# Low parts of the weights kept in DRAM from the first pass for the third

## The chip, the cores and the metric

The kernel runs on one core of a Trainium2 chip. The metric is the device time of one execution in microseconds. A core has five engines with queues of their own, each in order: TensorE (PE; its weight loads are shown as PEld), VectorE (DVE), ScalarE (ACT), GpSimd (POOL) and SyncE (SP). SyncE issues the ordinary transfers, GpSimd the indexed ones (gathers); the engines wait for each other and for transfers on semaphores.

## The reference

One decoder layer on `x` of 1024 tokens by 1024 columns, all in float32:

```
h = x + mixer(rms_norm(x))          # proj = xn @ w_in (3592 columns); gated conv, gated delta rule; @ w_out
h = h + cross(rms_norm(h), mem)     # q = xn @ w_xq, 4 heads over 256 memory tokens, @ w_xo
h = h + peer(rms_norm(h))           # q = xn @ w_pq; per token 8 heads x 16 of 16384 experts:
                                    #   sum_e gate_e * gelu(x . u_e) * v_e
out = rms_norm(h)
```

The delta rule is a recurrence over tokens, in blocks of 128. `expert_u` and `expert_v` have 16384 rows of 1024 numbers.

## The kernel before

**Products in two parts.** A float32 product is made of three matmuls in fp32r: with each operand split into a high part (its value rounded to fp32r) and a low part (the rest), `mm3` (L246) adds high x high (L248), and two products of a high with a low part (L249, L250). `load_w` (L237) brings one weight piece of 128 x 1024 numbers, 512 KB: SyncE loads it to `wraw` (L240), ScalarE copies it to `whi` (L242), VectorE subtracts, `wlo = wraw - whi` (L244). There are three `wraw` buffers, two `whi` and two `wlo`. A `whi` or `wlo` buffer comes free when the matmuls that read it are done; a `wraw` buffer when the copy and the subtraction are.

**Tokens in three passes.** `Chunk` ca is tokens 0 to 255 (two blocks), cb 256 to 767 (four), cc 768 to 1023 (two). Each pass reads the same weights: `inproj` 28 pieces of `w_in`, by `proj_ct` (L302); `outproj` 8 pieces of `w_out` and the end of `cross` 8 of `w_xo`, both by `split_proj` (L331) and `proj_tok` (L314); `cross` 8 pieces of `w_xq`; `queries` 8 of `w_pq`. That is 60 pieces in each pass. Between `inproj` and `outproj` lies the recurrence (`invert`, `recur`). The keys and values of the memory, `kmd` and `vmd`, are made once, during the first pass, and loaded again by `cross`.

**Experts in two ways.** For tokens 256 to 767 the layer is computed densely: `densify` (L1025) makes a table of gates for all experts from one-hot rows (VectorE L1050, L1051, L1053; TensorE L1059; ScalarE L1063; stored to `gd` by SyncE, L1066), and `dense` (L1068) runs over all 16384 experts, loading pieces of `u_t` and `expert_v` through `load_w`. For the other four blocks the chosen rows are gathered: 128 gathers of 128 rows of `expert_u` a block (L918, `gathered`), each reduced by VectorE (L935), then as many of `expert_v`, added by VectorE (L1020), or for block 0 by TensorE (L964, L971). They land in six `g` buffers.

**Order.** The program is written as generators that `merge` interleaves in given proportions: ca alone with the memory; cb with gathers; then `queries(cb)` with the start of cc; then the rest of cc with the tables of `densify`; at last `dense` with the gathers that are left. Buffers are handed out in that order. A planner then puts each engine's instructions into a fixed order, by a priority from the program's order (shifted by the offsets `PG1`, `PG2` and so on) and by simulated times; semaphores follow from the data. On the chip each queue keeps that order, SyncE's transfers included.

Of the kernel before, what the change touches and what calls it, by code (L numbers as in the profile page):

```python
# [9 lines left out]
F32 = mybir.dt.float32  # L10
# [10 lines left out]
P = 128  # L21
SEQ = 1024
D = 1024
KD = D // P
T = 512
# [17 lines left out]
G1, G2, G3, G4, G5 = 98, 90, 107, 17, 60  # L43
A5 = -1
C4, T5 = 61, 92
NSHORT, NRAW, NHI, NLO, NG, LU, LV, VD = 6, 3, 2, 2, 6, 1, 1, 194
PG1, PG2, PG3, PT, PR, PD = 100, -25, 0, 0, 0, 0


# [63 lines left out]
def _body(ctx, tc, I, out, dbg, front_only):  # L113
    nc = tc.nc
# [12 lines left out]
    dr = ctx.enter_context(tc.tile_pool(name="dr", bufs=1, space=bass.MemoryType.DRAM))  # L127
# [9 lines left out]
    def short():  # L137
        return dp.tile([P, T + 4], F32, name="d_s")
# [6 lines left out]
    def psum():  # L145
        banks["n"] += 1
        return pp.tile([P, T], F32, name="ps" if banks["n"] % 2 or not banks["both"] else "po")
# [14 lines left out]
    cs = constants()  # L162
# [55 lines left out]
    xnd = dr.tile([SEQ, D], F32, name="xnd")  # L218
    yd = dr.tile([SEQ, D], F32, name="yd")
    gd = dr.tile([T // 32, P, P, 32], F32, name="gd")  # L220


    def rsqrt(dst, ss, scale, eps, tag=""):
# [10 lines left out]
            tt(t, t, x, op=OP.mult)  # L234
            stt(dst if it == 2 else y, t, 1.5, y, op0=OP.add, op1=OP.mult)

    def load_w(src):  # L237

        raw = wp.tile([P, D], F32, name="wraw", bufs=NRAW)
        nc.sync.dma_start(raw if len(src.shape) == 2 else raw.rearrange("p (a c) -> p a c", a=2), src)  # L240
        hi = wp.tile([P, D], F32R, name="whi", bufs=NHI)
        act(hi, raw, AF.Copy)  # L242
        lo = wp.tile([P, D], F32R, name="wlo", bufs=NLO)
        tt(lo, raw, hi.bitcast(F32), op=OP.subtract)  # L244
        return hi, lo

    def mm3(ps, lh, ll, rh, rl, first, last, open_=False):
# [19 lines left out]
    class Parts:  # L267


        def __init__(self, units, per):  # L270
            self.units, self.per = units, per
# [27 lines left out]
                stt(xlo[:, k, :nt], ps[:, :nt], gain[:, k:k + 1], xhi[:, k, :nt].bitcast(F32),  # L299
                    op0=OP.mult, op1=OP.subtract)  # L300

    def proj_ct(src, x, nt):  # L302

        xhi, xlo = x
        ps = psum()
        hi, lo = load_w(src)
        for k in range(KD):
            js = slice(k * P, (k + 1) * P)
            mm3(ps[:, :nt], hi[:, js], lo[:, js], xhi[:, k, :nt], xlo[:, k, :nt], k == 0, k == KD - 1)
            if k % 4 == 3:  # L310
                yield
        return ps[:, :nt]

    def proj_tok(wsrc, lhs, nblk, consume):  # L314

        for half in range(2):
            pss = [psum() for b in range(nblk)]
            for k in range(KD):
                cs = slice(half * 512, (half + 1) * 512)
                if k % 2 == 0:  # L320
                    hi, lo = load_w(wsrc[k * P:(k + 2) * P, cs].rearrange("(a p) c -> p a c", a=2))
                ks = slice((k % 2) * 512, (k % 2 + 1) * 512)
                xh, xl = lhs(k)
                for b in range(nblk):
                    bs = slice(b * P, (b + 1) * P)
                    mm3(pss[b], xh[:, bs], xl[:, bs], hi[:, ks], lo[:, ks], k == 0, k == KD - 1)
                yield
            for b in range(nblk):
                consume(b, half, pss[b])

    def split_proj(wsrc, units, hv):  # L331

        nt = len(hv) * P
        xhi, xlo = split_parts(nt)
        for k in range(KD):
            src = units[k // 4][:, k % 4]
            act(xhi[:, k], src, AF.Copy)
            tt(xlo[:, k], src, xhi[:, k].bitcast(F32), op=OP.subtract)
        yield

        def put(b, half, ps):
            dst = hv[b][:, half * 512:(half + 1) * 512]
            tt(dst, ps, dst, op=OP.add)

        yield from proj_tok(wsrc, lambda k: (xhi[:, k], xlo[:, k]), len(hv), put)


    def memory():
# [23 lines left out]


    class Chunk:
        def __init__(self, b0, nb):
            self.b0, self.nb, self.t0, self.T = b0, nb, b0 * P, nb * P

        def half(self):
# [20 lines left out]
    def inproj(c):  # L399

        t0, NB, T = c.t0, c.nb, c.T
# [7 lines left out]
        x = split_parts(T)  # L409
        xhi, xlo = x  # L410
# [36 lines left out]
        for i in (1, 0, 2):  # L447
            dst_u = c.half()
            qkv.append(dst_u)
            for h in range(NH):  # L450
                j = 4 * i + h
                ps = yield from proj_ct(I["w_in"][12 + j], x, T)
                raw = short()[:, :T + 3]
                nc.vector.tensor_copy(raw[:, 0:3], halo_q[:, j])
                act(raw[:, 3:T + 3], ps, AF.Copy)
                nc.vector.tensor_copy(halo_q[:, j], raw[:, T:T + 3])
                a = dst_u[:, h]
                act(a, raw[:, 0:T], AF.Copy, scale=dw[:, j, 0:1])
                for k in range(1, 4):
                    stt(a, raw[:, k:T + k], dw[:, j, k:k + 1], a, op0=OP.mult, op1=OP.add)  # L460
                th = raw[:, 0:T]
                act(th, a, AF.Tanh, scale=0.5)
                stt(a, th, 1.0, a, op0=OP.add, op1=OP.mult)
                yield
# [33 lines left out]
        cb = c.small("cb")  # L498
# [13 lines left out]

        yc = c.half()
        for j in range(4):
            pc = yield from proj_ct(I["w_in"][4 + j], x, T)
            csb = short()[:, :T]
            act(csb, pc, AF.Copy)
            ph = yield from proj_ct(I["w_in"][8 + j], x, T)
            ch = short()[:, :T + 2]
            nc.vector.tensor_copy(ch[:, 0:2], halo_c[:, j])  # L520
            tt(ch[:, 2:T + 2], csb, ph, op=OP.mult)
            nc.vector.tensor_copy(halo_c[:, j], ch[:, T:T + 2])
            yield
            a = yc[:, j]
            act(a, ch[:, 0:T], AF.Copy, scale=cw[:, j, 0:1])
            stt(a, ch[:, 1:T + 1], cw[:, j, 1:2], a, op0=OP.mult, op1=OP.add)
            stt(a, ch[:, 2:T + 2], cw[:, j, 2:3], a, op0=OP.mult, op1=OP.add)
            pb = yield from proj_ct(I["w_in"][j], x, T)
            tt(yc[:, j], a, pb, op=OP.mult)
            yield  # L530

        zT = c.half()
        for h in range(NH):
            ps = yield from proj_ct(I["w_in"][24 + h], x, T)
            th = short()[:, :T]
            act(th, ps, AF.Tanh, scale=0.5)
            stt(zT[:, h], th, 1.0, ps, op0=OP.add, op1=OP.mult)
            yield
# [147 lines left out]
    def outproj(c):  # L686
        t0, NB, T = c.t0, c.nb, c.T
        for b in range(4):
            dbgout("yT", c.yc[:, b], (b, slice(None), slice(t0, t0 + T)))
            dbgout("yT", c.yd[:, b], (4 + b, slice(None), slice(t0, t0 + T)))  # L690
        c.h = rows(NB)
        for b in range(NB):
            nc.sync.dma_start(c.h[b], I["x"][t0 + b * P:t0 + (b + 1) * P])
        yield from split_proj(I["w_out"], [c.yc, c.yd], c.h)
        for b in range(NB):
            dbgout("h1", c.h[b], slice(t0 + b * P, t0 + (b + 1) * P))


    def cross(c):
        NB, T = c.nb, c.T  # L700
        hv = c.h
# [4 lines left out]
        x = split_parts(T)  # L706
        to_channels(x[0], x[1], xs, g_x)
        yield
        qx, ox = [], []
        pend = []  # L710

        def query(i):
            if i % 4 == 0:
                qx.append(c.half())
            ps = yield from proj_ct(I["w_xq"][i], x, T)
            act(qx[i // 4][:, i % 4], ps, AF.Copy)

        def scores(h):
# [45 lines left out]
        for h in range(4):  # L764
# [4 lines left out]
                yield from query(2 * h + 3)  # L769
            values(h, pr)  # L770
            yield
        yield from split_proj(I["w_xo"], ox, hv)
        for b in range(NB):
            dbgout("h2", hv[b], slice(c.t0 + b * P, c.t0 + (b + 1) * P))

# [1 line left out]
    def queries(c):  # L777

        t0, NB, T = c.t0, c.nb, c.T
        hv = c.h  # L780
        rstd = normalise(hv)
        gffn = unit().rearrange("p a t -> p (a t)")[:, :D]
        nc.sync.dma_start(gffn, I["g_ffn_row"].partition_broadcast(P))
        xs = rows(NB)
        for b in range(NB):
            tb = slice(t0 + b * P, t0 + (b + 1) * P)
            nc.sync.dma_start(hd2[tb], hv[b])
            stt(xs[b], hv[b], rstd[:, b:b + 1], gffn, op0=OP.mult, op1=OP.mult)
            nc.sync.dma_start(xnd[tb], xs[b])
            dbgout("xn", xs[b], tb)  # L790
        x = split_parts(T)
        to_channels(x[0], x[1], xs, None)
        yield
        for b in range(NB):
            routes[c.b0 + b] = Route(c.b0 + b)
        for hh in range(4):
            pair = []
            keys = sp.tile([P, 2, P], F32, name="keys")
            nc.sync.dma_start(keys, I["keysT"][:, 2 * hh:2 * hh + 2])
            for i in (2 * hh, 2 * hh + 1):  # L800
                ps = yield from proj_ct(I["w_pq"][i], x, T)
                pair.append(short()[:, :T])
                act(pair[-1], ps, AF.Copy)
                yield
            for b in range(0, NB, 2):
                yield from best_keys(c.b0 + b, hh, pair, keys, b * P)
# [349 lines left out]
            yield  # L1156


    ca, cb, cc = Chunk(0, 2), Chunk(2, 4), Chunk(6, 2)

    def recurrence(c):
        for b in range(0, c.nb, 2):
# [16 lines left out]


    run(inproj(ca))
    mem = memory()
    next(mem)
# [71 lines left out]

# [10 lines left out]
```

## Time and profile before

Three runs: 3332.52, 3342.78 and 3343.30 us, median 3342.78.

| of the profiled execution | |
|---|---|
| its own time | 3335.89 us |
| span, first to last instruction | 3334.1 us |
| mean granted TensorE clock | 0.908 |
| busy: PE / DVE / ACT / POOL | 84% / 81% / 40% / 40% |
| read from and written to HBM | 838.77 MB, 48.76 MB |
| L244, all low parts | 452, 552.4 us of VectorE |
| L242, all high parts | 452, 479.9 us of ScalarE |

The page gives each engine's busy time over the whole span. As the program has stages with different limits, the rows below cut the span into stretches (times from the span's start). A row of such a view has the stretch, its length, the busy time and the number of instructions of PE, PEld, DVE, ACT and POOL, the granted clock, the mean busy share of the 16 DMA engines, and GB/s. A row of waits reads: engine, output and line that waited, what it waited for, the sum in us, how often, the longest. SPq is SyncE's queue of transfers.

### The profile page before, as it was taken

The page shows a single profiled execution, that of the slowest core. Times are in us where ns is not written, and L with a number is a line of the kernel's source. Part 1 is how long each engine was busy: PE and PEld are TensorE (multiplying, and loading weights), DVE is VectorE, ACT ScalarE, POOL GpSimd, SP SyncE. Part 2 cuts the span into 40 slices and gives each one's busy share as a digit, 9 for nine tenths or more (in the row PEclk, how much of TensorE's full clock was granted, in tenths as well). Part 3 has the DMA queues.
Part 4 walks back from the last instruction along what each step waited for, and adds up shares of the span by engine and source line. Part 5 has one row for each costly group of instructions (what it writes and reads, how often), then busy time and mean ns, then how long its engine had stood idle before and what let it go on. Part 6 is the DMA issues. An engine that isn't in the chain of part 4 may idle for free.

```text
span 3334.1 us, 42650 instructions
## 1 busy us (share of the span) xinstructions
PE 2784.7 (84%) x14826; PEld 2307.0 (69%) x14826; DVE 2693.7 (81%) x5527; ACT 1339.8 (40%) x2367; POOL 1324.6 (40%) x1028
## 2 busy tenths in 40 slices
PE   7898588877888877466777999999999999999950
PEld 7887466666555656465656888888888888888840
DVE  6654899978655788997668999888888888887888
ACT  5444333322232323334443554444444444444430
POOL 0000046746545441000000456556655555665665
PEclk9999788989998888788788999999999999999975
DMA  4344368959988884113455889999999999999998
GB/s 166 113 147 140 120 233 302 354 184 324 328 309 306 308 291 155 64 77 143 154 190 188 297 307 363 347 344 346 345 336 342 348 348 349 343 339 339 348 329 315
DMA packets 325495, 890.34 MB, mean 267 GB/s; under 512 B 27424, under 2 KB 96672, under 8 KB 321184
## 3 DMA queue, kind: packets, MB, share of 16 engines
q0 software_dynamic: 147456, 536.94, 44.3%
q1 hardware_dynamic: 177824, 350.69, 30.0%
q8 instruction: 116, 1.90, 0.2%
q14 instruction: 99, 0.81, 0.1%
HBM read 838.77 MB, written 48.76 MB: 266 GB/s over the span
## 4 chain that ended last, share of the span: by engine, by line
PE 43%; DVE 3%; issue 2%; DMA 1%; ACT 1%; POOL 1%; SPq 0%; POOLq 0%; DVEq 0%; ACTq 0%
PE ps L248 7%; PE ps L249 7%; PE ps L250 7%; PE po L248 7%; PE po L250 7%; PE po L249 7%; DMA g<-expert_v,g_ii 1%; POOL g L918 1%; DVE unit L1053 0%; DMA d_s<-kmd 0%; PE ps L1059 0%; DVE g_y L1020 0%; DVE wlo L244 0%; ACT whi L242 0%; DVE unit L1050 0%
## 5 line engine op out<-in xcount | busy, mean ns | idle before, releaser
L918 POOL DMA_INDIRECT g<-expert_u,g_ii x512 | 666.4, 1302 | 898.9 <-DVE t_s L820 434.4
L918 POOL DMA_INDIRECT g<-expert_v,g_ii x384 | 518.5, 1350 | 930.8 <-ACT g L1001 536.0
L242 ACT ACTIVATE whi<-wraw 128x1024 fp32r<-128x1024 f32 x452 | 479.9, 1062 | 836.0 <-PE ps L249 413.5
L244 DVE TENSOR_TENSOR wlo<-wraw,whi 128x1024 fp32r<-128x1024 f32 x452 | 552.4, 1222 | 321.7 <-ACT whi L242 319.4
L935 DVE SCALAR_TENSOR_TENSOR g<-g,xn 128x1024 f32<-128x1024 f32 x512 | 617.4, 1219 | 121.0 <-DMA g<-expert_u,g_ii 111.7
L250 PE MATMUL ps<-unit,wlo 128*128 128x512 f32 (+1 forms) x1784 | 653.3, 367 | 39.4 <-DVE wlo L244 39.3
L248 PE MATMUL ps<-unit,whi 128*128 128x512 f32 (+1 forms) x1784 | 659.1, 370 | 13.7 <-ACT whi L242 5.5
L249 PE MATMUL ps<-unit,whi 128*128 128x512 f32 (+1 forms) x1784 | 651.6, 365 | 0.0
L1020 DVE SCALAR_TENSOR_TENSOR g_y<-g,g_a,g_y 128x1024 f32<-128x1024 f32 x381 | 488.1, 1281 | 20.1 <-DMA g<-expert_v,g_ii 12.7
L249 PE MATMUL po<-wlo,unit 128*128 128x512 f32 x1136 | 444.0, 391 | 0.0
L250 PE MATMUL po<-whi,unit 128*128 128x512 f32 x1136 | 443.9, 391 | 0.0
L250 PEld LDWEIGHTS ps<-unit,wlo 128*128 128x128 f32 x1784 | 350.3, 197 | 98.6 <-DVE wlo L244 45.0
L248 PEld LDWEIGHTS ps<-unit,whi 128*128 128x128 f32 x1784 | 351.6, 197 | 76.7 <-ACT whi L242 11.0
L249 PEld LDWEIGHTS ps<-unit,whi 128*128 128x128 f32 x1784 | 351.5, 197 | 50.0 <-issue 0.8
L248 PE MATMUL po<-whi,unit 128*128 128x512 f32 x1136 | 383.1, 391 | 0.0
L249 PEld LDWEIGHTS po<-wlo,unit 128*128 128x128 f32 x1136 | 214.1, 188 | 48.3 <-issue 2.7
L250 PEld LDWEIGHTS po<-whi,unit 128*128 128x128 f32 x1136 | 214.0, 188 | 46.8 <-issue 2.5
L248 PEld LDWEIGHTS po<-whi,unit 128*128 128x128 f32 x1136 | 214.0, 188 | 45.8 <-issue 1.1
L1113 ACT ACTIVATE unit<-po 128x512 f32<-128x512 f32 x256 | 152.6, 597 | 150.1 <-PE po L250 144.8
L964 POOL DMA_INDIRECT g<-expert_v,g_y x128 | 139.4, 1089 | 161.3 <-DVE g L935 57.5
L1100 ACT ACTIVATE po<-unit 128x512 f32<-128x512 f32 x248 | 144.5, 605 | 0.0
L1059 PE MATMUL ps<-unit 128*128 128x128 f16 x1024 | 86.8, 239 | 52.3 <-DVE unit L1053 38.7
(391 smaller groups left out, 4053.1 us busy)
## 6 DMA issues: line engine op xcount, KB each, us to landing
wraw<-u_t SPq DMA_DIRECT2D x128, 512.0 KB, 7.1
wraw<-expert_v SPq DMA_DIRECT2D x128, 512.0 KB, 7.0
wraw<-w_in SPq DMA_DIRECT2D x84, 512.0 KB, 4.6
gd<-unit SPq DMA_DIRECT2D x32, 1024.0 KB, 5.9
unit<-gd SPq DMA_DIRECT2D x32, 1024.0 KB, 15.1
wraw<-w_out SPq DMA_DIRECT2D x24, 512.0 KB, 4.2
wraw<-w_xq SPq DMA_DIRECT2D x24, 512.0 KB, 4.4
wraw<-w_xo SPq DMA_DIRECT2D x24, 512.0 KB, 4.9
```

Of the source, the lines that this page charges most:

```text
L242: act(hi, raw, AF.Copy)
L244: tt(lo, raw, hi.bitcast(F32), op=OP.subtract)
L248: nc.tensor.matmul(ps, lh, rh, start=first, stop=False, skip_group_check=open_)
L249: nc.tensor.matmul(ps, lh, rl, start=False, stop=False, skip_group_check=open_)
L250: nc.tensor.matmul(ps, ll, rh, start=False, stop=last, skip_group_check=open_)
L918: nc.gpsimd.indirect_dma_start(out=g, out_offset=None, in_=I[table], in_offset=bass.IndirectOffsetOnAxis(ap=ii[:, k:k + 1], axis=0))
L935: stt(g, g, 1.0, xn, op0=OP.mult, op1=OP.mult, accum_out=r.a[:, k:k + 1])
L964: nc.gpsimd.indirect_dma_start(out=g, out_offset=None, in_=I["expert_v"], in_offset=bass.IndirectOffsetOnAxis(ap=iT[:, t:t + 1], axis=0))
L1020: stt(y, g, a[:, k:k + 1], y, op0=OP.mult, op1=OP.add)
L1059: nc.tensor.matmul(ps[:, u * P:(u + 1) * P], part[i][:, g, :, t], oj[:, g, :, t], start=i == 0, stop=i == 1)
L1100: act(pss[b], y[b][:, half * 512:(half + 1) * 512], AF.Copy)
L1113: act(y[b][:, half * 512:(half + 1) * 512], pss[b], AF.Copy)
```

## The change

`load_w` gets a key: a pass and the name of the piece. In the first pass ("save") the low part is stored, after the subtraction, into a DRAM tile `lod` of 60 slots, by SyncE. In the third pass ("use") there is no subtraction; the low part is loaded from its slot into `wlo` by SyncE. The second pass, the memory's weights and the dense stage have no key and do as before. There are four `wraw` and four `wlo` buffers instead of three and two; `whi` keeps two. For the 12 KB a partition that they take, the area of the on-chip memory that the program sets aside for its dynamic DMAs (the gathers) is given as 4096 bytes a partition.

```diff
-NSHORT, NRAW, NHI, NLO, NG, LU, LV, VD = 6, 3, 2, 2, 6, 1, 1, 194
+NSHORT, NRAW, NHI, NLO, NG, LU, LV, VD = 6, 4, 2, 4, 6, 1, 1, 194
...
+    lod = dr.tile([60, P, D], F32, name="lod")
...
-    def load_w(src):
+    parts_of = {}
+
+    def load_w(src, key=None):
...
         lo = wp.tile([P, D], F32R, name="wlo", bufs=NLO)
+        keep, *piece = key or (None,)
+        if keep == "use":
+            nc.sync.dma_start(lo.bitcast(F32), lod[parts_of[tuple(piece)]])
+            return hi, lo
         tt(lo, raw, hi.bitcast(F32), op=OP.subtract)
+        if keep == "save":
+            n = parts_of.setdefault(tuple(piece), len(parts_of))
+            nc.sync.dma_start(lod[n], lo.bitcast(F32))
         return hi, lo
...
-    def proj_ct(src, x, nt):
+    def proj_ct(src, x, nt, key=None):
...
-    def proj_tok(wsrc, lhs, nblk, consume):
+    def proj_tok(wsrc, lhs, nblk, consume, key=None):
...
-                    hi, lo = load_w(wsrc[k * P:(k + 2) * P, cs].rearrange("(a p) c -> p a c", a=2))
+                    hi, lo = load_w(wsrc[k * P:(k + 2) * P, cs].rearrange("(a p) c -> p a c", a=2),
+                                    key and (*key, half, k))
...
-                ps = yield from proj_ct(I["w_in"][12 + j], x, T)
+                ps = yield from proj_ct(I["w_in"][12 + j], x, T, (c.keep, "w_in", 12 + j))
...
-    ca, cb, cc = Chunk(0, 2), Chunk(2, 4), Chunk(6, 2)
+    ca, cb, cc = Chunk(0, 2, "save"), Chunk(2, 4), Chunk(6, 2, "use")
...
-    nc = bacc.Bacc("TRN2", target_bir_lowering=False, num_devices=1)
+    nc = bacc.Bacc("TRN2", target_bir_lowering=False, num_devices=1, dynamic_dma_scratch_size=4096)
```

## Rows read from the trace of the kernel before

**Rows 1.** Busy time of every engine by stretch (PE, PEld, DVE, ACT, POOL).
```profile
0.00:430.00 430.00, 347.90 (x2382) 325.08 (x2382) 286.35 (x869) 189.11 (x371) 0.20 (x4) 0.90 0.39 133
...
1050.00:1350.00 300.00, 233.24 (x1375) 183.00 (x1373) 241.79 (x918) 95.42 (x159) 105.66 (x95) 0.84 0.71 256
1350.00:1540.00 190.00, 105.80 (x846) 95.70 (x847) 177.91 (x519) 69.74 (x194) 0.00 (x0) 0.74 0.17 67
1540.00:1780.00 240.00, 176.34 (x1314) 146.96 (x1313) 166.21 (x338) 108.48 (x281) 0.00 (x0) 0.85 0.51 188
...
1850.00:3200.00 1350.00, 1350.00 (x5956) 1117.57 (x5955) 1142.39 (x1395) 655.83 (x948) 769.62 (x558) 1.00 0.95 341
3200.00:3334.00 134.00, 10.66 (x47) 8.46 (x46) 115.05 (x151) 10.97 (x19) 85.70 (x72) 0.55 0.86 310
```

**Rows 2.** Waits in 1050 to 1350 us.
```profile
DVE g L935 <- DMA g<-expert_u,g_ii: 35.1, 20, 4.3
...
PE ps L250 <- DVE wlo L244: 24.6, 7, 11.7
...
PE ps L971 <- DMA g<-expert_v,g_y: 22.4, 7, 6.3
...
DVE wlo L244 <- ACT whi L242: 15.5, 10, 4.4
```

**Rows 3.** Waits in 1540 to 1780 us, and a group of TensorE there with idle time.
```profile
DVE wlo L244 <- ACT whi L242: 44.4, 15, 6.7
...
ACT whi L242 <- PE ps L250: 33.0, 13, 5.9
...
PE ps L1059 <- DVE unit L1053: 16.3, 10, 5.9
...
PE ps L729 <- DMA d_s<-kmd: 9.4, 2, 4.8
...
L249 PE MATMUL ps<-wlo,unit 128*128 128x512 f32 x59 | 24.6, 417 | 4.0 <-DVE wlo L244 4.0
```

**Rows 4.** The subtraction L244 by stretch: VectorE busy (count), clock, DMA share, GB/s.
```profile
0.00:430.00 430.00, 95.44 (x78) 0.90 0.39 133
...
1050.00:1350.00 300.00, 47.30 (x39) 0.84 0.71 256
...
1540.00:1780.00 240.00, 34.22 (x28) 0.85 0.51 188
```

**Rows 5.** Tile wlo in a stretch of 50 us: PE, PEld, DVE, clock, DMA, GB/s.
```profile
1050.00:1100.00 50.00, 12.97 (x33) 6.00 (x32) 4.89 (x4) 0.83 0.97 375
```

**Rows 6.** Transfers by SyncE: count, KB each, median us from issue to landing.
```profile
wraw<-w_in SPq DMA_DIRECT2D x84, 512.0 KB, 4.6
...
xnd<-unit SPq DMA_DIRECT2D x8, 512.0 KB, 6.2
```

**Rows 7.** One issue in SyncE's queue: start, duration us, line.
```profile
1555.77 0.33 SPq L240 DMA_DIRECT2D wraw<-w_xq  x1
```

**Rows 8.** Waits of SyncE's queue: 0 to 430 us, then 1540 to 1780 us.
```profile
SPq L240 <- DVE wlo L244: 123.4, 47, 14.1
...
SPq L240 <- DVE wlo L244: 147.1, 20, 28.8
SPq L1066 <- ACT unit L1063: 40.4, 13, 10.9
```

**Rows 9.** Waits in the dense stage, 1900 to 3200 us.
```profile
ACT whi L242 <- PE ps L249: 227.5, 88, 3.9
...
DVE wlo L244 <- ACT whi L242: 175.1, 153, 3.3
...
ACT whi L242 <- DMA wraw<-expert_v: 18.7, 9, 5.8
```

**Rows 10.** Line L1020 by stretch, the last one: VectorE busy (count).
```profile
3200.00:3334.00 134.00, 97.37 (x76) 0.55 0.86 310
```

**Rows 11.** The longest wait in 1780 to 1850 us.
```profile
POOL g L918 <- ACT g L1001: 535.0, 1, 535.0
```

More of the change, by code (lines that the diff above doesn't have):

```diff
@@ L300, in to_channels @@
                     op0=OP.mult, op1=OP.subtract)
-    def proj_ct(src, x, nt):
+    def proj_ct(src, x, nt, key=None):
         xhi, xlo = x
         ps = psum()
-        hi, lo = load_w(src)
+        hi, lo = load_w(src, key)
         for k in range(KD):
@@ L329, in proj_tok, with split_proj @@
                 consume(b, half, pss[b])
-    def split_proj(wsrc, units, hv):
+    def split_proj(name, units, hv, keep):
         nt = len(hv) * P
@@ L343, in put @@
             tt(dst, ps, dst, op=OP.add)
-        yield from proj_tok(wsrc, lambda k: (xhi[:, k], xlo[:, k]), len(hv), put)
+        yield from proj_tok(I[name], lambda k: (xhi[:, k], xlo[:, k]), len(hv), put, (keep, name))
     def memory():
@@ L374, in _body, with __init__ @@
     class Chunk:
-        def __init__(self, b0, nb):
+        def __init__(self, b0, nb, keep=None):
+            self.keep = keep
             self.b0, self.nb, self.t0, self.T = b0, nb, b0 * P, nb * P
@@ L514, in inproj @@
         for j in range(4):
-            pc = yield from proj_ct(I["w_in"][4 + j], x, T)
+            pc = yield from proj_ct(I["w_in"][4 + j], x, T, (c.keep, "w_in", 4 + j))
             csb = short()[:, :T]
             act(csb, pc, AF.Copy)
-            ph = yield from proj_ct(I["w_in"][8 + j], x, T)
+            ph = yield from proj_ct(I["w_in"][8 + j], x, T, (c.keep, "w_in", 8 + j))
             ch = short()[:, :T + 2]
@@ L527, in inproj @@
             stt(a, ch[:, 2:T + 2], cw[:, j, 2:3], a, op0=OP.mult, op1=OP.add)
-            pb = yield from proj_ct(I["w_in"][j], x, T)
+            pb = yield from proj_ct(I["w_in"][j], x, T, (c.keep, "w_in", j))
             tt(yc[:, j], a, pb, op=OP.mult)
@@ L533, in inproj @@
         for h in range(NH):
-            ps = yield from proj_ct(I["w_in"][24 + h], x, T)
+            ps = yield from proj_ct(I["w_in"][24 + h], x, T, (c.keep, "w_in", 24 + h))
             th = short()[:, :T]
@@ L693, in outproj @@
             nc.sync.dma_start(c.h[b], I["x"][t0 + b * P:t0 + (b + 1) * P])
-        yield from split_proj(I["w_out"], [c.yc, c.yd], c.h)
+        yield from split_proj("w_out", [c.yc, c.yd], c.h, c.keep)
         for b in range(NB):
@@ L714, in query @@
                 qx.append(c.half())
-            ps = yield from proj_ct(I["w_xq"][i], x, T)
+            ps = yield from proj_ct(I["w_xq"][i], x, T, (c.keep, "w_xq", i))
             act(qx[i // 4][:, i % 4], ps, AF.Copy)
@@ L771, in cross @@
             yield
-        yield from split_proj(I["w_xo"], ox, hv)
+        yield from split_proj("w_xo", ox, hv, c.keep)
         for b in range(NB):
@@ L800, in queries @@
             for i in (2 * hh, 2 * hh + 1):
-                ps = yield from proj_ct(I["w_pq"][i], x, T)
+                ps = yield from proj_ct(I["w_pq"][i], x, T, (c.keep, "w_pq", i))
                 pair.append(short()[:, :T])
```

## The prediction

> **What bounds the kernel now.** I read the stages first, then who waits in two of them, then SyncE's queue and the transfers. [rows 1] cut the span at the places where the work changes. From 0 to 430 us the first pass runs nearly alone: TensorE 348 of 430 us busy, VectorE 286, DMA 0.39. From 430 to 1050 the second pass shares the core with the expert gathers. The third pass, 60 weight pieces, lies between 1050 and 1780 in three parts: 1050 to 1350 (stretch A: its input projection, the second pass's queries, gathers), 1350 to 1540 (recurrence, routing and `densify`; VectorE 178 of 190 us) and 1540 to 1780 (stretch B: output projection, cross attention, queries, and the rest of `densify`). From 1850 to 3200 the dense stage has TensorE at 1350 of 1350 us at full clock with DMA at 0.95. After it VectorE still has 76 gathered rows to add, 97.4 of the last 134 us. The reader is to see that no engine is full in A (TensorE 233 of 300, VectorE 242) nor in B (176 of 240, VectorE 166), so what the third pass is worth is read from the waits there.
>
> In A TensorE stands 24.6 us waiting for the low part of a weight; VectorE stands 15.5 us for the high part before it can subtract, 35.1 us for gathers, and TensorE 22.4 us for gathers [rows 2]. In B the same subtraction holds VectorE 44.4 us, because ScalarE's high copy waits 33.0 us for TensorE to free a buffer; VectorE runs in order, so `densify` stands behind it, and TensorE in turn waits 16.3 us for `densify` and 4.0 us for low parts [rows 3]. That is the loop which the change cuts in one place.
>
> **The change part by part.**
>
> *Subtractions that go.* [rows 4] count 39 subtractions in A and 28 in B, and one lies between; eight of A's belong to the second pass's `w_pq`, which leaves 31 + 1 + 28 = 60. At 47.30/39 = 1.21 us A loses 37.6 us of VectorE's work, B 34.2, together with the one between 73 us. With the waits in front of them (15.5 and 44.4) VectorE is relieved of 53.1 us in A and 78.6 in B. These are upper ends: where VectorE alone sets the pace, the stretch shortens by all of it, but no further than TensorE's idle time there, 66.8 us in A and 63.7 in B [rows 1].
>
> *Stretch A.* Nearest to the path is the 24.6 us of TensorE; that goes if the loaded low part is there in time. Against it stand 31 more transfers of 0.524 MB, 16.3 MB; at the dense stage's 341 GB/s they take 48 us of the DMA's time and raise its share from 0.71 to about 0.87 [rows 1]. The waits on gathers are 35.1 + 22.4 = 57.5 us; if they grow as the share does, by 0.22, that is 12.7 us back. I take 24.6 - 12.7 = 12 us gained. Ends: 53 gained if VectorE paces all of it; 33 lost if the gather waits double and only the 24.6 is won. The trace shows the DMA at 375 GB/s in 1050 to 1100 us [rows 5], so a short stretch can go above the dense stage's rate. The Trainium skill (DMA: Bandwidth & Descriptors, section Where 436 GB/s comes from) says that a core's traffic with HBM is bound at about 358 GB/s, which that row exceeds. By the page those 50 us have no room at all, and 375 + 54 - 358 = 71 GB/s would come some 10 us later (an estimate from the page's figure); A would gain 2 us instead of 12, and the sum below would be 10 us higher. The measured row decides, and the sum goes by it.
>
> *Stretch B.* DMA has room: 28 transfers, 14.7 MB, 43 us, from 0.51 to 0.69. The low end is what TensorE itself waits for, 4.0 + 16.3 = 20 us; the high end 63.7. Late next, once the subtraction is gone, are ScalarE's high copies, which still have two buffers and still wait for TensorE (33.0 us), and the loads of `kmd`, on which TensorE waits 9.4 us [rows 3]. These don't get shorter, so I take 25, near the low end.
>
> *Between 1350 and 1540* there is one subtraction; VectorE is full of other work. Nothing.
>
> *Stores in the first pass.* 60 stores of 512 KB. No such store exists before; the nearest is `xnd`, same size, 6.2 us to landing [rows 6]. SyncE issues them in its own queue, 0.33 us each [rows 7], 20 us altogether in 430. Each waits for its subtraction, and behind it stand the next raw loads, the `kmd` stores and the loads of `x`. But a raw load waits for a subtraction already, because that frees its buffer: 47 such waits, 123.4 us, in this stretch [rows 8]. With four raw buffers the load behind a store waits for the same or an earlier subtraction, so the store makes nothing later. A low buffer is now held until the store has landed; with 78 subtractions in 430 us [rows 4] four buffers give 22 us, against 6.2. 31.5 MB more raise 133 GB/s to 206 [rows 1]. I cost it at nothing; without that cover it is at most the 20 us of issues.
>
> *Loads in the third pass.* Each load waits for a low buffer, which the piece four before frees on TensorE, while the high copy waits for the piece two before. It is therefore asked for early: with 39 pieces in A's 300 us, two pieces are 15 us, against a landing of 4.6 us for `wraw` [rows 4, 6]. Queued behind it in SyncE are the next raw load, `gd` stores and `kmd`. SyncE waits 147.1 us for subtractions in B as it is [rows 8]; those waits turn into waits on the high copy, which comes sooner. Nothing; the upper bound, a whole landing exposed, is the slower rival below.
>
> *Buffers elsewhere.* The dense stage and second pass keep the subtraction. There the high copy has two buffers as before: ScalarE waits 227.5 us for TensorE and VectorE 175.1 us for ScalarE, but only 18.7 us for a raw weight [rows 9]. A low part can't be ahead of its high part, so two more low buffers stay empty, and a fourth raw one can save no time on a TensorE that is never idle. What it can do is move the gathers against the products: 76 rows are left over, 97.37/76 = 1.28 us each [rows 10]; fifteen more or fewer is 20 us either way, which I keep for the range.
>
> *The 4 KB scratch* touches only the 1024 gathers. In the dense stage one costs GpSimd 769.6/558 = 1.38 us, and 580 us of idle time there would hide a longer one. In the tail 72 issues are 85.7 of 134 us; half as long again they would nearly fit [rows 1]. Nothing; the upper end is that half, 43 us, if none of it is hidden in the tail.
>
> **Sum.** The profiled execution took 3335.9 us, 1.8 more than its span of 3334.1. 3335.9 - 12 - 25 = 3299. The end follows the third pass because both things that come last start behind it: the dense stage's products, and the gathers, which stood 535 us before they went on, just before the dense stage [rows 11]. The profiled execution is 6.9 us under the median of the three runs (3342.8); I add half of that and predict 3302.
>
> **The rivals.**
>
> *VectorE paces both stretches.* Then the relief counts in full up to TensorE's idle time: about 53 + 64, less the 12.7 of gathers, 104 us: 3232. For it: VectorE is busy or stuck on a subtraction in 211 of B's 240 us. Against: in A it also waits for gathers.
>
> *The end does not follow.* The dense stage starts 37 us earlier, but the gathers restart when they did, and the tail of 134 us grows by as much: 3336. What released them is block 0's last addition on ScalarE after third-pass routing, which speaks against it; that VectorE still has 97 us of rows to add when TensorE is done speaks for it.
>
> *The loaded low part comes late (slower).* SyncE's queue is in order; a low load behind a `gd` store (13 waits, 40.4 us in B [rows 8]) is issued late, and TensorE then waits for a whole landing of 4.6 us that a subtraction of 1.2 us never cost. From 37/4.6 = 8 of the 60 pieces on the gain is gone; at one piece in four it is 15 x 4.6 = 69 us lost, 3299 + 69 = 3368. For it: TensorE already waits for `kmd`, whose loads pass through the same queue [rows 3]. Against: four low buffers and the idle DMA in B.
>
> *The scratch throttles gathers.* 3299 + 43 = 3342 at worst. For it: the area is the one thing in the change that all gathers share. Against: the idle time above.
>
> **How the numbers follow.** Forecast 0.50 (3270 to 3326); VectorE paces 0.12; the end does not follow 0.14; low part late 0.20; scratch 0.04. The range reaches from 3238 (most of the first rival) to 3370 (the slower one). A difference of 0.3%, 10 us, is about what can be told from none. Faster holds the forecast nearly whole, the first rival and a little of the third: 0.62. Same: most of the third and the forecast's upper end, 0.14. Slower 0.24.
>
> **What would show it.** In the changed profile: 60 subtractions fewer at the same 1.21 to 1.22 us; TensorE's wait for low parts in A gone, and no wait for a load in its place; VectorE's wait on the high copy in B gone; the dense stage's first product some 37 us earlier and its length the same within 10; the tail still about 134 us. TensorE waiting for `wlo` from DMA, a longer first pass, or longer waits for gathers in A would prove me wrong.

## The result, and the profile after

The changed kernel takes 3284.6 us (median of 4 runs, 3280.9 to 3289.1) against 3343.0 before: a ratio of 0.9837, 95% interval 0.9820 to 0.9854. That is 58 us less by the medians and 54 by the ratio; 41 were forecast. The profiled execution took 3286.0 us, with a span of 3283.9, 50 less than the one before.

Where the time went is read from seven marks that both traces have: the first load of `w_in` for the second and for the third pass, the first one-hot comparison of `densify`, the end of the recurrence, the first Gelu of the dense stage, the last product, and the end. Lengths in us between them:

| | first pass | second pass | third: input projection | recurrence | third: rest | dense stage | tail | span |
|---|---|---|---|---|---|---|---|---|
| before | 359 | 694 | 312 | 164 | 297 | 1385 | 123 | 3334 |
| changed | 365 | 690 | 270 | 163 | 288 | 1389 | 119 | 3284 |

The input projection of the third pass gives 42 us and the rest of that pass 9. The dense stage and the tail keep their lengths within 4 us and start earlier. The first pass got 6 us longer.

Busy time by stretch in the changed kernel, the columns as in [rows 1]; then the input projection between its own marks, in the changed kernel (270 us) and in the kernel before (312 us):

```profile
0.00:430.00 430.00, 342.18 (x2359) 317.80 (x2360) 278.73 (x845) 188.42 (x370) 0.20 (x4) 0.91 0.57 207
...
1050.00:1290.00 240.00, 211.61 (x1311) 166.31 (x1310) 193.22 (x801) 88.36 (x148) 93.24 (x87) 0.92 0.95 359
```

```profile
1055.00:1325.00 270.00, 221.35 (x1380) 172.36 (x1378) 224.84 (x947) 98.06 (x161) 102.26 (x94) 0.89 0.92 345
```

```profile
1053.00:1365.00 312.00, 231.03 (x1362) 181.73 (x1360) 253.76 (x968) 97.73 (x162) 105.56 (x94) 0.82 0.68 245
```

In the projection TensorE is now busy 82% of the time (221 of 270 us) against 74%, at a granted clock of 0.89 instead of 0.82. VectorE has 225 us of work against 254, and its idle time fell from 58 to 45 us. The DMA's share is 0.92 instead of 0.68; from 1050 to 1290 us it moves 359 GB/s. The first pass, with the stores, moves 207 GB/s (206 were forecast).

TensorE's groups in 1050 to 1350 us of the changed kernel (line, shapes, count, busy and mean, then idle time before the group and what ended it), and then one of the waits there:

```profile
L261 PE MATMUL ps<-unit,wlo 128*128 128x256 f32 (+1 forms) x288 | 91.2, 319 | 2.6 <-DVE wlo L252 2.6
...
L984 PE MATMUL ps<-g,g_y 128*32 128x512 f32 x208 | 33.6, 674 | 3.4 <-DMA g<-expert_v,g_y 3.3
```

```profile
DVE g L948 <- DMA g<-expert_u,g_ii: 21.8, 11, 4.0
```

Against [rows 2], TensorE's wait for low parts fell from 24.6 to 2.6 us. Its wait for gathers fell as well, from 22.4 to 3.3, and VectorE's from 35.1 to 21.8, although the DMA is busier. The two waits of TensorE together are 41 us shorter. That this is nearly what the projection lost is in part chance: by the two rows above TensorE's idle time fell by 32 us in all (81 to 49), as other waits grew, and its busy time by 10, at the higher granted clock. What the clock has in the gain was not separated.

Waits in the last part of the third pass, 1490 to 1728 us, and SyncE's queue in a piece of it (start, duration, line):

```profile
ACT whi L246 <- issue: 33.0, 14, 3.9
...
PE ps L1072 <- DVE unit L1066: 18.2, 11, 5.3
...
PE ps L742 <- DMA d_s<-kmd: 13.3, 3, 6.2
```

```profile
1579.71 0.32 SPq L250 DMA_DIRECT2D wlo<-lod  x1
1580.74 0.38 SPq L244 DMA_DIRECT2D wraw<-w_xo  x1
1581.84 0.80 SPq L1079 DMA_DIRECT2D gd<-unit  x2
1582.68 1.36 SPq L733 DMA_DIRECT2D d_s<-kmd  x1
```

VectorE's 44.4 us on the high copy [rows 3] are gone, but TensorE's waits are no shorter: 18.2 for `densify` (16.3 before), 13.3 for `kmd` (9.4 before). Each of the four `kmd` loads comes out behind a low load, and two of them behind a low load, a raw load and two stores, as here. ScalarE has 33 us before its high copies for which the profile names no releaser.

The transfers on the page of the changed kernel (count, KB, median us to landing):

```profile
wraw<-w_in SPq DMA_DIRECT2D x84, 512.0 KB, 6.0
...
lod<-wlo SPq DMA_DIRECT2D x60, 512.0 KB, 4.2
wlo<-lod SPq DMA_DIRECT2D x60, 512.0 KB, 6.0
```

A store lands in 4.2 us, a low load in 6.0; `w_in` itself lands later than the 4.6 us of [rows 6].

### The profile page after: what moved, and what is told of

Its sections match the earlier page's. It is cut to its first block, busy times and chain, and to the rows that moved or that the text cites. A ratio compares the mean times of both kernels' runs of the same rounds, so it can differ in the third digit from the quotient of the medians.

```text
span 3283.9 us, 42835 instructions
## 1 busy us (share of the span) xinstructions
PE 2767.8 (84%) x14826; PEld 2291.6 (70%) x14826; DVE 2626.9 (80%) x5467; ACT 1343.9 (41%) x2367; POOL 1330.5 (41%) x1028
## 4 chain that ended last, share of the span: by engine, by line
PE 51%; DVE 12%; issue 4%; DMA 4%; ACT 2%; POOL 1%; SPq 0%; POOLq 0%; DVEq 0%; ACTq 0%
PE ps L259 9%; PE ps L261 9%; PE ps L260 9%; PE po L260 7%; PE po L261 7%; PE po L259 7%; DMA g<-expert_u,g_ii 1%; DVE unit L1066 1%; POOL g L931 1%; PE ps L1072 1%; DVE t_s L832 1%; DVE unit L1064 1%; DMA g<-expert_v,g_ii 1%; DVE g L948 1%; DVE unit L1063 1%
## 5 line engine op out<-in xcount | busy, mean ns | idle before, releaser
L252 DVE TENSOR_TENSOR wlo<-wraw,whi 128x1024 fp32r<-128x1024 f32 x392 | 479.2, 1223 | 280.2 <-ACT whi L246 275.4
L259 PE MATMUL ps<-unit,whi 128*128 128x512 f32 (+1 forms) x1784 | 651.2, 365 | 17.2 <-ACT whi L246 7.9
L261 PE MATMUL ps<-unit,wlo 128*128 128x512 f32 (+1 forms) x1784 | 644.7, 362 | 9.2 <-DVE wlo L252 9.2
L260 PE MATMUL ps<-unit,whi 128*128 128x512 f32 (+1 forms) x1784 | 644.3, 361 | 0.0
L1033 DVE SCALAR_TENSOR_TENSOR g_y<-g,g_a,g_y 128x1024 f32<-128x1024 f32 x381 | 488.0, 1281 | 18.2 <-DMA g<-expert_v,g_ii 11.3
L259 PEld LDWEIGHTS ps<-unit,whi 128*128 128x128 f32 x1784 | 345.0, 193 | 76.6 <-ACT whi L246 13.8
L260 PEld LDWEIGHTS ps<-unit,whi 128*128 128x128 f32 x1784 | 344.7, 193 | 49.9 <-issue 1.7
L261 PE MATMUL po<-unit,wlo 128*128 128x256 f32 (+1 forms) x360 | 124.8, 347 | 25.7 <-DVE wlo L252 25.7
```

What stands on the lines that cost most here:

```text
L259: nc.tensor.matmul(ps, lh, rh, start=first, stop=False, skip_group_check=open_)
L260: nc.tensor.matmul(ps, lh, rl, start=False, stop=False, skip_group_check=open_)
L261: nc.tensor.matmul(ps, ll, rh, start=False, stop=last, skip_group_check=open_)
L1033: stt(y, g, a[:, k:k + 1], y, op0=OP.mult, op1=OP.add)
```

## The experiments

All ratios are to the kernel before, run on the same chip at the same time, with 95% intervals; the diffs are against the changed kernel. The lengths of the stages, in the columns of the table above, are from the profiled execution of each:

| | ratio | first | second | input proj. | recurrence | rest | dense | tail | span |
|---|---|---|---|---|---|---|---|---|---|
| buffers only | 0.9985 (0.9970 to 1.0001) | 351 | 688 | 319 | 164 | 296 | 1386 | 121 | 3325 |
| stores only | 1.0008 (0.9995 to 1.0022) | 362 | 689 | 314 | 164 | 298 | 1388 | 122 | 3337 |
| loads, old buffers | 1.0016 (1.0004 to 1.0029) | 373 | 692 | 298 | 165 | 306 | 1389 | 119 | 3342 |
| four low, three raw | 0.9938 (0.9917 to 0.9959) | 368 | 703 | 268 | 167 | 290 | 1390 | 115 | 3301 |
| w_in only | 0.9866 (0.9846 to 0.9886) | 349 | 692 | 277 | 164 | 298 | 1385 | 121 | 3286 |
| all but w_in | 0.9976 (0.9960 to 0.9992) | 366 | 688 | 316 | 164 | 291 | 1389 | 114 | 3328 |
| load and subtract | 1.0008 (0.9992 to 1.0023) | 366 | 685 | 306 | 166 | 302 | 1387 | 121 | 3333 |
| gd by ScalarE | 0.9861 (0.9840 to 0.9883) | 369 | 685 | 268 | 163 | 295 | 1389 | 116 | 3285 |
| second pass too | 0.9891 (0.9870 to 0.9912) | 371 | 698 | 267 | 177 | 288 | 1389 | 117 | 3307 |
| stores by GpSimd | 0.9826 (0.9806 to 0.9845) | 361 | 685 | 274 | 165 | 291 | 1389 | 118 | 3283 |
| kmd by GpSimd | 0.9789 (0.9758 to 0.9820) | 364 | 681 | 274 | 164 | 277 | 1389 | 115 | 3264 |
| the same in two passes | 0.9802 (0.9786 to 0.9817) | 358 | 696 | 279 | 168 | 278 | 1389 | 117 | 3285 |

The second pass, whose source is the same in all but one of them, is 681 to 703 us long: that is how far one profiled execution of a newly planned program can differ in a stage that was not edited. Executions of one program differ as well: those of the last one in the table took 3263 to 3287 us, and the profiled one is the slowest of them. Differences of a few us in one stage are not read.

**The parts of the change.** Four runs take it apart: the buffers without stores and loads, the stores and loads with the old buffers, and `w_in` alone against all the rest.

```diff
-    ca, cb, cc = Chunk(0, 2, "save"), Chunk(2, 4), Chunk(6, 2, "use")
+    ca, cb, cc = Chunk(0, 2), Chunk(2, 4), Chunk(6, 2)
```

> Four raw and four low buffers and the 4 KB scratch, but nothing stored and nothing loaded: all three passes subtract as in the kernel before. Theory (the third pass gains because its subtractions leave VectorE): within 0.3% of before, 3333 to 3353 us, with TensorE's wait for low parts between 1050 and 1350 us still about 20 to 30 us. Rival (the deeper buffers and the order that the planner makes of them bring the gain): 3310 us or less.

```diff
-NSHORT, NRAW, NHI, NLO, NG, LU, LV, VD = 6, 4, 2, 4, 6, 1, 1, 194
+NSHORT, NRAW, NHI, NLO, NG, LU, LV, VD = 6, 3, 2, 2, 6, 1, 1, 194
...
-    nc = bacc.Bacc("TRN2", target_bir_lowering=False, num_devices=1, dynamic_dma_scratch_size=4096)
+    nc = bacc.Bacc("TRN2", target_bir_lowering=False, num_devices=1)
```

> Stores and loads as in the change, but three raw and two low buffers and the scratch as before. Theory: the subtractions are gone, but a low part with two buffers is asked for only when the piece two before is done, so part of the gain is lost to landings of some 6 us; 3290 to 3325 us. Rival (buffers bring the gain): no better than before, 3333 us or more. If it equals the change within 0.3%, the buffers are worth nothing.

```diff
         keep, *piece = key or (None,)
+        if piece and piece[0] != "w_in":
+            keep = None
```

> The change, but only the 28 pieces of w_in are stored and loaded; the other 32 subtract in every pass. The traces of before and after put 42 of the 50 us at the start of the recurrence, that is, behind w_in. Theory by these traces: 3295 to 3305 us, about 40 us of the gain. Rival, the sum as predicted (12 us in the first stretch, 25 in the last): some 3330 us.

```diff
         keep, *piece = key or (None,)
+        if piece and piece[0] == "w_in":
+            keep = None
```

> The change, but w_in is subtracted in every pass; only w_out, w_xq, w_xo and w_pq are stored and loaded (32 pieces). Theory by the traces: the last stretch is held by the loads of kmd behind the gd stores in SyncE's queue and gains some 10 us, so 3328 to 3340 us. Rival, the sum as predicted: 25 us, 3318 us. The two gains of this and the run with w_in alone should add up to the whole change, if the parts are independent.

Measured: 3334.2 us (buffers only), 3342.6 (old buffers), 3291.6 (`w_in` only; 3295 to 3305 were forecast), 3330.0 (all but `w_in`), beside 3336.3 for the kernel before. The two selections add up: 0.0134 + 0.0024 = 0.0158 of 0.0163 for the whole. So 82% of the gain comes from 28 of the 60 pieces, and the sum as predicted, which gave more to the last stretch, falls. Neither the buffers nor the loads bring anything alone, and the forecast of 3290 to 3325 us for the old buffers missed. With those buffers the input projection is 14 us shorter than before (298 against 312), but the first pass is 14 longer and the rest of the third pass 9. There one group of TensorE in 1050 to 1350 us and one wait of 0 to 430 us read:

```profile
L261 PE MATMUL ps<-unit,wlo 128*128 128x256 f32 (+1 forms) x280 | 91.5, 329 | 18.4 <-DMA wlo<-lod 10.1 <-DVE wlo L252 8.3
```

```profile
DVE wlo L252 <- DMA lod<-wlo: 20.8, 15, 2.5
```

TensorE now waits for the loaded low part itself, and in the first pass VectorE waits for stores to land before it may write a low buffer again. The buffers are what makes the loads early.

**VectorE's time, or TensorE's order?** The change removes work from VectorE and also a dependence of TensorE on it. This run puts the work back and leaves TensorE's wait for the low part out.

```diff
         if keep == "use":
             nc.sync.dma_start(lo.bitcast(F32), lod[parts_of[tuple(piece)]])
+            tt(raw, raw, hi.bitcast(F32), op=OP.subtract)
             return hi, lo
```

> The change, but in the third pass VectorE also makes the subtraction, into the raw buffer, where nobody reads it; TensorE uses the loaded low part. So VectorE's 73 us and its waits for the high part are back, and only TensorE's wait for VectorE is cut. Theory 1 (the gain is that TensorE no longer waits for VectorE in its order: 24.6 us for low parts, and the waits for gathers behind it): most of the gain stays, 3290 to 3310 us. Theory 2 (the gain is VectorE's 73 us): it goes, 3325 us or more.

3338.3 us, ratio 1.0008: the gain is gone. Groups of VectorE and TensorE in 1050 to 1350 us of this run:

```profile
L251 DVE TENSOR_TENSOR wraw<-wraw,whi 128x1024 f32<-128x1024 f32 x29 | 35.1, 1217 | 3.9 <-ACT whi L246 3.9
```

```profile
L260 PE MATMUL ps<-unit,whi 128*128 128x256 f32 (+1 forms) x280 | 92.9, 333 | 17.3 <-ACT whi L246 11.6 <-DVE d_s L535 4.1 <-DVE unit L551 1.1
```

29 subtractions whose result nobody reads, 35.1 us, make the input projection 306 us long, 36 more than the 270 of the change. Its row between its marks:

```profile
1051.00:1357.00 306.00, 228.97 (x1374) 176.88 (x1373) 258.07 (x979) 99.27 (x163) 104.57 (x97) 0.83 0.83 309
```

VectorE has 258 us of work here, 33 more than with the change, and 48 us of idle time against 45: the projection grew by VectorE's work. So the gain needs the subtractions off VectorE, and theory 1 as it was put falls. But the run does not cut TensorE loose from VectorE altogether. A raw buffer is now held until its subtraction is done; SyncE's raw loads wait 42.3 us for that, and TensorE waits 11.6 us for high parts (1.6 with the change) and 5.9 for loaded low parts. VectorE's work and that hold were not separated. Nor is VectorE's time enough by itself: with the old buffers it has as little work (224 us), and the projection takes 298 us.

**Which buffers.**

```diff
-NSHORT, NRAW, NHI, NLO, NG, LU, LV, VD = 6, 4, 2, 4, 6, 1, 1, 194
+NSHORT, NRAW, NHI, NLO, NG, LU, LV, VD = 6, 3, 2, 4, 6, 1, 1, 194
```

> The change, with three raw buffers as before and four low ones. With three raw and two low the change gained nothing (1.0016); TensorE then waited 10.1 us for loaded low parts and VectorE 20.8 us for stores in the first pass. Theory (the low buffers decide, since they set how early a low part is asked for): within 0.3% of the change, 3275 to 3294 us. Rival (the fourth raw buffer decides, since raw loads stand behind low loads in SyncE's queue): 3310 us or more.

3311.1 us: between the two theories, and neither is borne out. By the ratios the two low buffers are worth 0.0078 (1.0016 to 0.9938) and the fourth raw one 0.0101 (0.9938 to 0.9837), while without the loads all of them together bring nothing that can be told from the spread. The input projection has its whole gain with three raw buffers (268), so there the low ones decide; what is lost against the change shows in the second pass (703 against 690), and 703 is also the end of the spread named above. The profiled execution is the fastest of four, so it shows 17 us of the loss. In that second pass TensorE's idle time is as in the change (144 and 146 us) and its busy time 15 us longer, 13 of them in the products with gathered rows (L984, 51 against 38 us). What the fourth raw buffer does there stays open.

**The last stretch.** Two runs move transfers out of SyncE's queue.

```diff
-                nc.sync.dma_start(gd[4 * n + q, :, 64 * e:64 * e + 64], st[e])
+                nc.scalar.dma_start(gd[4 * n + q, :, 64 * e:64 * e + 64], st[e])
```

> The change, with the 32 gd stores of densify issued from ScalarE's queue, right behind the copies that fill them, not from SyncE's. In the last stretch kmd's loads stand behind these stores in SyncE's queue, and TensorE waits 13.3 us for kmd. Theory (the queue holds this stretch): 10 to 25 us faster than the change, 3260 to 3275 us. Rival (the chain through softmax and ScalarE's copies holds it, and issues now cost ScalarE time): 3280 to 3295 us.

```diff
-            nc.sync.dma_start(km, kmd[h])
+            (nc.gpsimd if c.keep == "use" else nc.sync).dma_start(km, kmd[h])
...
-            nc.sync.dma_start(vh, vmd[h])
+            (nc.gpsimd if c.keep == "use" else nc.sync).dma_start(vh, vmd[h])
```

> The change, with the third pass's eight loads of kmd and vmd issued by GpSimd, not by SyncE, where they stand behind gd stores that wait for ScalarE. Theory (kmd's late landing holds the last stretch; TensorE waits 13.3 us for it there): 8 to 20 us faster than the change, 3264 to 3277 us. Rival (when kmd comes earlier, softmax and densify hold TensorE instead, as with the gd stores moved): 3280 to 3290 us.

With the stores moved, nothing: 3287.4 us, and TensorE waits for `kmd` exactly as long; its group in 1490 to 1730 us of that run, and a piece of SyncE's queue:

```profile
L742 PE MATMUL ps<-d_s,unit 128*128 128x256 f32 x32 | 13.9, 593 | 13.5 <-DMA d_s<-kmd 13.3 <-ACT unit L1076 0.2
```

```profile
1577.90 0.32 SPq L250 DMA_DIRECT2D wlo<-lod  x1
1578.88 0.38 SPq L244 DMA_DIRECT2D wraw<-w_xo  x1
1579.31 0.46 SPq L733 DMA_DIRECT2D d_s<-kmd  x1
```

The load stands behind the low and the raw load of the next piece all the same. In every profiled execution without low loads in this stretch (the kernel before, buffers only, stores only, `w_in` only) TensorE waits 9.3 to 9.6 us for `kmd`; in every one with them, and with `kmd` on SyncE, 12.7 to 15.4. Moved to GpSimd, whose queue has no gather ready then, it is issued when its buffer is free (GpSimd's instructions of that run, in brackets the idle time before each and what ended it):

```profile
1579.50 0.54 POOL L733 DMA_DIRECT2D d_s<-kmd  x1 [2.07 <-PE ps L1072]
1592.65 0.54 POOL L759 DMA_DIRECT2D d_s<-vmd  x1 [12.62 <-PE ps L764]
```

TensorE's wait for `kmd` is gone from that stretch, the stretch is 277 us long instead of 288, and the kernel takes 3265.6 us (one of its four executions 3281.8), 0.9789 of before against the change's 0.9837; the last run of the table, which has the same edit, takes 0.9802 (0.9786 to 0.9817). Of the 20 us by which its span is shorter than the change's, 11 are there; 9 show in the second pass, which was not edited, and are not explained.

**The first pass.**

```diff
-    ca, cb, cc = Chunk(0, 2, "save"), Chunk(2, 4), Chunk(6, 2, "use")
+    ca, cb, cc = Chunk(0, 2, "save"), Chunk(2, 4), Chunk(6, 2)
```

> The change's buffers and its 60 stores in the first pass, but the third pass subtracts and loads nothing. In the traces the second pass's first weight is loaded at 351 us with the buffers alone, at 349 with the 28 stores of w_in, at 366 with the other 32 and at 365 with all. Theory (the stores of w_out, w_xq, w_xo and w_pq cost the first pass some 14 us): that load at 363 to 368 us and 3342 to 3352 us in all. Rival, as predicted (stores cost nothing): as the buffers alone, 3334 us, within 0.3%.

```diff
-            nc.sync.dma_start(lod[n], lo.bitcast(F32))
+            nc.gpsimd.dma_start(lod[n], lo.bitcast(F32))
```

> The change, with the 60 stores issued by GpSimd, which has nothing else to do in the first pass, not by SyncE. Theory (a store waits in SyncE's queue for VectorE and the loads behind it with it): the first pass is 10 to 14 us shorter and the whole 3268 to 3276 us. Rival (the low buffer held until its store has landed, or the DMA's load, costs the time): the same as the change, 3280 to 3290 us.

Stores only (the third pass without "use") takes 3341.7 us, 0.2% more than the buffers only and just short of the 3342 that was forecast, and the first pass 362 us instead of 351; with only the stores of `w_in` it takes 349. So the other 32 stores cost the first pass some 11 us. Issued by GpSimd they cost the same (361 us, 3284.0 in all), so the stores' place in SyncE's queue is not the reason. TensorE waits 7.8 us for `kmd` in 200 to 360 us of the changed kernel, 6.5 with stores only, 5.9 with stores by GpSimd, but 1.1 with the buffers only. The last run takes `kmd` away from SyncE there too (its diff is against the run with `kmd` by GpSimd):

```diff
-            (nc.gpsimd if c.keep == "use" else nc.sync).dma_start(km, kmd[h])
+            (nc.gpsimd if c.keep else nc.sync).dma_start(km, kmd[h])
...
-            (nc.gpsimd if c.keep == "use" else nc.sync).dma_start(vh, vmd[h])
+            (nc.gpsimd if c.keep else nc.sync).dma_start(vh, vmd[h])
```

> As the run before, with kmd and vmd issued by GpSimd in the first pass too, where TensorE waits 7.8 us for kmd in the changed kernel and GpSimd has no work. Theory (a kmd load behind other transfers in SyncE's queue costs the first pass as it did the third): some 5 to 8 us less than the 3265.6 us of that run, a ratio to before of 0.975 to 0.978. Rival (the first pass is held by its weights): 0.979 as before it.

The first pass is 358 us long, 6 less than with `kmd` on SyncE, but the whole is no faster (0.9802, an interval that holds 0.9789), so the forecast of 0.975 to 0.978 missed. In the profiled execution, the slowest of five, the second pass is 696 us against 681. What else the stores cost is open.

**More of the same in the second pass.**

```diff
-    ca, cb, cc = Chunk(0, 2, "save"), Chunk(2, 4), Chunk(6, 2, "use")
+    ca, cb, cc = Chunk(0, 2, "save"), Chunk(2, 4, "use"), Chunk(6, 2, "use")
```

> The change, with the second pass loading the low parts as well: 60 subtractions fewer, 73 us of VectorE, which is busy 494 of 620 us there and nearly all the time from 450 to 700. Theory by the first stretch of the third pass (TensorE waits for low parts behind VectorE): 20 to 50 us faster than the change, 3235 to 3265 us. Rival (the gathers hold this stretch, and 31.5 MB more at a DMA share of 0.82 slow them): no faster than the change, 3284 us or more.

3299.4 us, 15 more than the change. One of its waits in 370 to 1060 us:

```profile
DVE g L948 <- DMA g<-expert_u,g_ii: 105.5, 58, 5.7
```

VectorE has 505 us of work there instead of 564, but waits 105.5 us for gathers, 75.9 in the change: half of the 59 us that it is spared goes into that wait. The second pass is 8 us longer, and the third pass's recurrence 14, into which 14 gathers now fall instead of 3. The rival's number is right; that the gathers hold this stretch is read from these waits and was not tested.

## Why the prediction was right or wrong, point by point

- *The kind and place of the gain*: right. The third pass is shorter, the dense stage and the tail follow unchanged. The rival that the end does not follow falls: the gathers' long stand, 436 us now, ended with the third pass again, and the tail is 119 us against 123.
- *Stretch A, 12 us*: wrong; it is the term that was mis-sized, 42 measured. The step that failed is "nearest to the path is the 24.6 us of TensorE", less 12.7 for gather waits that grow with the DMA's share. Putting VectorE's work back costs 36 us there for 35.1 us of work, so VectorE's work set the length of A, in its own time or through the buffers that it holds, and the upper end, 53, was the nearer one. That is the mechanism of the first rival, which had a chance of 0.12. The gather waits did not grow but fell, 57.5 to 25.1 us, with the DMA at 359 instead of 293 GB/s from 1050 to 1290 us, so the 12.7 had the wrong sign. Nor does the length hang on them: with `w_in` only TensorE waits 21.9 us for gathers, as before, and the projection is 35 us shorter all the same.
- *Stretch B, 25 us*: wrong; 9 measured. Of what was named as late next, `kmd` was the right one and was priced too low: 9.4 us became 13.3, since low loads came to stand in front of it. ScalarE's high copies did not wait less either (44 us before and after, 33 of them now without a named releaser). So the first rival's 64 us for B fail.
- *The two errors partly cancel*: 37 forecast, 52 measured in the third pass (42, 1 and 9), less 6 in the first. A came out 30 us above its term and B 16 below, so that the total is nearer to the result than its terms is luck.
- *The 358 GB/s of the Trainium skill* (DMA: Bandwidth & Descriptors, section Where 436 GB/s comes from) would have made A worth 2 us. A ran at 359 GB/s for 240 us, at 396 in the last 40 of them, and still gained 42: the trace goes above the figure, and it was not what held A.
- *The stores at nothing*: wrong by 6 us, or 14 against the buffers alone. The argument on SyncE's queue held for the stores themselves (GpSimd does no better); the term of at most 20 us for issues was not the one that counted. Some 6 us go when `kmd` leaves SyncE's queue in the first pass; the rest is open.
- *Loads asked for early*: right with four low buffers (no wait of TensorE for `lod` in A with the change), and wrong with two, where 10.1 us of it appear and the gain is gone. The slower rival, a late low part, is what that run shows.
- *Buffers elsewhere and the scratch at nothing*: right within 0.3%, 0.9985 for both together. Beside the loads the fourth raw buffer is worth 0.0101, for which the sum had no term.

## What to carry to other kernels

Where no engine is full, ask what one freed microsecond of each would move: here VectorE at 81% was the pace, since the gain went when its work was put back. The likely reason, not shown by itself, is that its queue held up TensorE at several places, of which the wait for low parts was one. A value that is loaded and not computed needs enough buffers to cover its landing, or its wait comes back under another name. Whatever is added to a transfer queue delays the small load that is already late in it: look for that one first, and give it a queue that is idle.

## What was not expected of the hardware

The DMA moved 359 GB/s over 240 us with 25.1 us of waits for gathers, against 57.5 in the kernel before, where it moved 293 GB/s in the same 240 us. Taking the gathers' area from the usual size to 4096 bytes changed nothing that can be seen: a gather of `expert_u` takes GpSimd 1.31 us and lands in about 7 us in the changed kernel, 1.30 and 7 before. And a `kmd` load of 256 KB issued by GpSimd takes 0.54 to 0.59 us of its queue, no more than the same load takes of SyncE's in the changed kernel (0.41 to 1.43, median 0.62).
